# A hybrid attention, scan and expert layer: the decay of the scan's carried states moved from C to the product of states and C

## The chip, the cores and the metric

One core of a Trainium2 chip runs the whole layer in one launch. The metric is the device time of that launch in microseconds (us): the median of three runs for each kernel, and beside it one profiled execution from which every row here is taken. Engines in the rows: PE is TensorE's matmuls, PEld its weight loads, DVE VectorE, ACT ScalarE, POOL GpSimd, SP the queue that issues most of the DMAs.

## The reference

The layer norms 1024 latent and 256 context tokens of width 1024, projects them with one weight `w_in`, runs differential attention and a two-directional Mamba-2 scan (SSD) in parallel, merges the two and ends with a mixture of experts. The change touches the scan alone. For each of 16 heads (64 channels, 4 groups of 4 heads), each chunk and each direction the reference computes

```python
y_diag = einsum('bcign,bcjgn->bcijg', cc, bc) * decay * dtc @ xc          # inside a chunk
y_off  = einsum('bcign,cbgrpn,bcigr->bcigrp', cc, h_prev, exp(acum))      # what earlier chunks carry in
y      = y_diag + y_off                                                   # + d * x, gated by silu(z), group norm
```

`acum` is the running sum of dt times a, `h_prev` the state (128 x 64 for a head) that enters the chunk, and `cc` is C, shared by the four heads of a group. `exp(acum)` depends on head and token i alone, so it may stand at C or at the product of the states and C.

## The kernel before, in words

The program is written out by a list scheduler. `Flow` (class at the top of the listing) keeps a model clock for each engine; pieces of work are Python generators ("streams") with a priority, each `yield` names what the next instructions need, and the stream whose needs are met first by the model is written next. The order of the instructions on every engine is therefore fixed when the kernel is built, from modelled durations; on the chip each engine runs its list in order and waits on semaphores.

`mixer_t` (L791) holds the projections that feed the scan, and the scan. `server` (L947, priority 3, the lowest) multiplies the projections, job by job: dt, 16 convolution tiles, 8 z tiles and 16 gate tiles, three fp32r matmuls of 512 columns for each k into the banks `acc`. It is what PE does when no stream of the scan is ready. `conv_post` and `gate_post` empty those banks on ACT and DVE. When the four convolution tiles of a group of heads are there, `group` (L992) runs, one group at a time, since its buffers `xn`, `Bn`, `hp0`, `hp1` and `CB` exist once:

- transposes of x and B, then `states` (L1050) for the two directions: `xw` on POOL, a matmul, four DVE updates of `hp` for each chunk; then CB = B C for eight chunks.
- four turns (2 pairs of heads x 2 halves of 512 tokens). In each, `unit` (L1080) runs for the two heads hh of the pair: two loads `R[d]` of the cumulated decay (one row of `acd` spread over 128 partitions, 256 KB each), W = mask times dt on DVE (4 + 4 small instructions), G = R[0] - ac on POOL, four DVE instructions that take the minimum with R[1] - ac, W times CB on POOL, exp(G) on ACT, W times G on DVE.
- beside it `decays` (L1129): exp(R[d]) on ACT, then R[d] times C on POOL, for both directions, so four of each in a turn.
- `products` (L1113): for each of four chunks and each head three matmuls into one bank `py`, accumulated there: W against xn, and R[0], R[1] against `hp0`, `hp1`. A head fills 64 of the 128 columns, and each fp32 matmul is two instructions in the trace: 48 in a turn. Model slack: 400 ns after the last of W and R.
- `evac` (L1137): y = d x + py on DVE, y times silu(z) on DVE; `norm` (L1153) after four turns.

Rings: R 6 buffers, W 2, G 2, yt 4, py 2 banks. W is freed by `products`, so the next turn's W starts behind this turn's matmuls. When all four groups are normed, `branches` (L1196) starts to load operands for the branch projections (`bacc` matmuls; `PACE` lets three tiles of 24 matmuls run before attention), and `attention_ahead` (L1326) loads the q and k of attention once five of those operands are there and no job is left.

Of the kernel before, what the change touches and what calls it, by code (L numbers as in the profile page):

```python
# [14 lines left out]
ALU = mybir.AluOpType  # L15
# [4 lines left out]
P = 128  # L20
D = 1024
KC = 8
T = 1024
# [3 lines left out]
LAM_INIT = 0.2  # L27
ND, NR, NDR, NA = 2, 4, 2, 5
LEAD = 2
SLACK = 400.0, 0.0, 200.0, 0.0, 800.0, 400.0, 1500.0  # L30
FG = 3, 3, 2
TAIL = "a0 a1 a2 a3 r0 s0 a4 s1 a5 s2 a6 r1 s3 a7 s4 s5 r2 s6 s7"
# [43 lines left out]
def _n(ap):  # L76
    return ap.tensor.name
# [299 lines left out]
class Layer:  # L377
# [413 lines left out]
    def mixer_t(s):  # L791
        tc, nc, I, F = s.tc, s.nc, s.I, s.F
# [6 lines left out]
        sp = s.open("sp", side="right")  # L799
        pp, pq = s.open("mixps", True), s.open("mixqs", True, side="right")  # L800
        mp = sp
        if True:
            acc = s.ring(pp, [P, 512], "acc", 4)
            aux = s.ring(pq, [P, 512], "aux", 2)
            pys = s.ring(pq, [P, 512], "py", 2)
# [8 lines left out]
            hcs = s.ring(sp, [P, 256], "hc", 2)  # L814
            xws = s.ring(sp, [P, 4, 64], "xw", 2)
            CBs = s.ring(sp, [P, 8, P], "CB", 1)
            Rs = s.ring(sp, [P, 512], "R", 6)
            Gs = s.ring(sp, [P, 4, P], "G", 2)
            Ws = s.ring(sp, [P, 4, P], "W", 2)
            dcol, db = s.dcol, s.db  # L820
            dtn = mp.tile([P, 2, 10, 32], F32, name="dtn")
            dt, dtd = dtn[:, 0], dtn[:, 1]
# [169 lines left out]
            def group(g, x0, x1, B, C):  # L992
                x = (x0, x1)
                yield [lambda: state["dt"], xns, Bns]
                xn, Bn = xns.get(), Bns.get()
                for c in range(0, 10, 2):
                    yield [x0, x1, aux]
                    pt = aux.get()
                    for i in range(2):
                        for q in range(2):  # L1000
                            F.tp(pt[:, (i * 2 + q) * P:(i * 2 + q + 1) * P], x[q][:, (c + i) * P:(c + i + 1) * P], s.ident)
                    yield [pt, "ANY"]
                    F.copy(xn[:, c:c + 2].rearrange("p a b -> p (a b)"), pt)
                    aux.put(pt)
                uxs.put(*x)
                for c in range(0, 10, 4):
                    n = min(4, 10 - c)
                    yield [B, aux]
                    pt = aux.get()
                    for i in range(n):  # L1010
                        F.tp(pt[:, i * P:(i + 1) * P], B[:, (c + i) * P:(c + i + 1) * P], s.ident)
                    yield [pt, "ANY"]
                    F.copy(Bn[:, c:c + n].rearrange("p a b -> p (a b)"), pt[:, :n * P])
                    aux.put(pt)
                yield [hps[0], hps[1], hcs]
                hp = [q.get() for q in hps]
                done, left = [], [16]
                for d in range(2):
                    F.spawn(0, states(g, d, xn, Bn, hp[d], done))
                yield [CBs]  # L1020
                CB = CBs.get()
                for half in range(2):
                    yield [C, B, aux]
                    pt = aux.get()
                    for i in range(4):
                        c = 2 + half * 4 + i
                        F.mm(pt[:, i * P:(i + 1) * P], B[:, c * P:(c + 1) * P], C[:, (c - 2) * P:(c - 1) * P], True, True)
                    yield [pt, "ANY"]
                    F.copy(CB[:, half * 4:half * 4 + 4].rearrange("p a b -> p (a b)"), pt)
                    aux.put(pt)  # L1030
                uBs.put(B)
                yt = {}
                for pair in range(2):
                    for half in range(2):
                        yield [pys]
                        py, ready = pys.get(), []
                        for hh in range(2):
                            yield [(Rs, 2), "NOW"]
                            F.spawn(0, unit(g, pair, half, hh, CB, C, ready))
                        F.spawn(1, products(g, pair, half, xn, hp, py, done, ready, yt))  # L1040
                yield [lambda: len(yt) == 4, "NOW"]
                xns.put(xn)
                Bns.put(Bn)
                for d in range(2):
                    hps[d].put(hp[d])
                CBs.put(CB)
                uCs.put(C)
                yield from norm(g, yt)
# [28 lines left out]
                hcs.put(*hc)  # L1077
                done.append(d)

            def unit(g, pair, half, hh, CB, C, ready):  # L1080

                r = 2 * pair + hh
                h = 4 * g + r
                t0 = 512 * half
                R = [Rs.get(), Rs.get()]
                for d in range(2):
                    F.dma(R[d], bass.AP(tensor=s.acd[d].tensor, offset=s.acd[d].offset + h * T + t0, ap=[[0, P], [1, 512]]))
                Rv = [q.rearrange("p (c i) -> p c i", i=P) for q in R]
                yield [Gs, Ws, "DVE"]
                G, W = Gs.get(), Ws.get()  # L1090
                cs = range(4 * half, 4 * half + 4)
                for c in range(4):
                    F.ts(W[:, c], s.le, dt[:, 2 + cs[c], h:h + 1], None, ALU.mult)
                for c in range(4):
                    F.stt(W[:, c], s.ge, dt[:, 2 + cs[c], 16 + h:16 + h + 1], W[:, c], ALU.mult, ALU.add)
                yield [R[0], "POOL"]
                F.ptt(G, Rv[0], ac[:, 0, 2 + 4 * half:6 + 4 * half, h:h + 1].to_broadcast([P, 4, P]), ALU.subtract)
                yield [G, R[1], "DVE"]
                for c in range(4):
                    F.stt(G[:, c], Rv[1][:, c], ac[:, 1, 2 + cs[c], h:h + 1], G[:, c], ALU.subtract, ALU.min)  # L1100
                k = []
                F.spawn(0, decays(R, C[:, t0:t0 + 512], k, F.clk["DVE"] + 100.0))
                yield [CB, W, "POOL"]
                F.ptt(W, W, CB[:, 4 * half:4 * half + 4], ALU.mult)
                yield [G, "ACT"]
                F.act(G, G, AF.Exp)
                yield [G, "DVE"]
                F.tt(W, W, G, ALU.mult)
                Gs.put(G)
                yield [lambda: len(k) == 2]  # L1110
                ready.append((hh, W, *R))

            def products(g, pair, half, xn, hp, py, done, ready, yt):  # L1113

                yield [lambda: len(done) == 2 and len(ready) == 2]
                yield [hp[0], hp[1], *(F.ready[_n(q)] + 400.0 for v in ready for q in v[1:])]
                for c in range(4):
                    n = 4 * half + c
                    for i, src in enumerate((xn[:, 2 + n], hp[0][:, n], hp[1][:, n])):
                        for v in ready:  # L1120
                            o = 64 * v[0]
                            x = 128 * pair + o
                            F.mm(py[o:o + 64, c * P:(c + 1) * P], src[:, x:x + 64], v[1 + i].rearrange("p c i -> p (c i)")[:, c * P:(c + 1) * P] if i == 0 else v[1 + i][:, c * P:(c + 1) * P], i == 0, i == 2, 134.5)
                for _, W, R0, R1 in ready:
                    Rs.put(R0, R1)
                    Ws.put(W)
                yield from evac(g, pair, half, py, yt)

            def decays(R, C, k, at):  # L1129
                for q in R:  # L1130
                    yield [q, at, "ACT"]
                    F.act(q, q, AF.Exp)
                    yield [q, "POOL"]
                    F.ptt(q, q, C, ALU.mult)
                    k.append(1)

            def evac(g, pair, half, py, yt):  # L1137
                sl = slice(512 * half, 512 * half + 512)
                yield [yts, "NOW"]
                y = yts.get()  # L1140
                F.dma(y, s.xT[2 * g + pair][:, sl])
                yield [y, py, "DVE"]
                F.stt(y, y, dcol[:, 2 * g + pair:2 * g + pair + 1], py, ALU.mult, ALU.add)
                pys.put(py)
                yield [lambda: 2 * g + pair in state["z"], zgs, "NOW"]
                z = zgs.get()
                F.dma(z, s.zs[2 * g + pair][:, sl])
                yield [z, "DVE"]
                F.tt(y, y, z, ALU.mult)
                zgs.put(z)  # L1150
                yt[pair, half] = y
# [192 lines left out]
    def attention(s):  # L1344
        tc, nc, F = s.tc, s.nc, s.F
        ap, pp = s.open("at"), s.open("aps", True)
        if True:
# [20 lines left out]
            def main():  # L1368
# [4 lines left out]
                plan = PLAN.split("|")  # L1373
                for p in range(len(pairs) + LEAD + 1):
                    for j in range(4):
                        for op in plan[j].split():
                            n = p - LEAD * (op[0] != "S") - (op[-1] == "'")
                            if 0 <= n < len(pairs):
# [1122 lines left out]
```

## Time and profile before

| | |
|---|---|
| median of 3 runs | 2750.43 us (2750.11 to 2753.43) |
| profiled execution | 2762.38 us, span in the trace 2760.1 us |
| mean granted TensorE clock | 0.979 of full speed |
| PE busy | 95% of the span |
| DVE, ACT, POOL busy | 73%, 49%, 33% |
| chain that ended last | PE 63%, DMA 8%, DVE 8% |

The profiled execution is 0.4% longer than the median, so a difference worked out from its rows is carried over to the median as it is. The scan lies between about 400 and 1050 us; attention follows to 1500 us, then the merge and the experts.

### The profile page before, as it was taken

The page shows a single profiled execution, that of the slowest core. Times are in us where ns is not written, and L with a number is a line of the kernel's source. Part 1 is how long each engine was busy: PE and PEld are TensorE (multiplying, and loading weights), DVE is VectorE, ACT ScalarE, POOL GpSimd, SP SyncE. Part 2 cuts the span into 40 slices and gives each one's busy share as a digit, 9 for nine tenths or more (in the row PEclk, how much of TensorE's full clock was granted, in tenths as well). Part 3 has the DMA queues.
Part 4 walks back from the last instruction along what each step waited for, and adds up shares of the span by engine and source line. Part 5 has one row for each costly group of instructions (what it writes and reads, how often), then busy time and mean ns, then how long its engine had stood idle before and what let it go on. Part 6 is the DMA issues. An engine that isn't in the chain of part 4 may idle for free.

```text
span 2760.1 us, 41127 instructions
## 1 busy us (share of the span) xinstructions
PE 2610.2 (95%) x14561; PEld 2099.0 (76%) x14561; DVE 2012.4 (73%) x4680; ACT 1341.9 (49%) x2104; POOL 920.9 (33%) x669
## 2 busy tenths in 40 slices
PE   7999999999999998999999999899999999999992
PEld 4888878878787776888888778677787787777771
DVE  6878133777776657888896657877879898888864
ACT  4211113344444446666675432335566666666652
POOL 0111010445354531000000000044667766777761
PEclk9999999999999999999999999999999999999996
DMA  7767253242425345322422872468999999999998
GB/s 275 226 205 220 62 149 102 69 145 77 138 77 149 91 120 186 119 86 87 142 97 75 263 252 107 168 234 288 292 319 315 339 333 311 315 314 307 296 308 251
DMA packets 275409, 545.67 MB, mean 198 GB/s; under 512 B 31562, under 2 KB 166835, under 8 KB 248194
## 3 DMA queue, kind: packets, MB, share of 16 engines
q1 hardware_dynamic: 238178, 432.95, 46.0%
q0 software_dynamic: 35872, 105.88, 14.7%
q10 hardware_dynamic: 1152, 4.19, 0.4%
q8 instruction: 115, 1.88, 0.3%
q14 instruction: 92, 0.75, 0.1%
HBM read 433.78 MB, written 124.73 MB: 202 GB/s over the span
## 4 chain that ended last, share of the span: by engine, by line
PE 63%; DMA 8%; DVE 8%; issue 3%; POOL 2%; ACT 2%; SPq 0%; ACTq 0%; POOLq 0%; DVEq 0%
PE gu L149 18%; PE acc L149 11%; PE dn L149 9%; PE bacc L149 6%; PE sps L149 5%; PE pv L149 4%; PE xt L153 3%; DMA cr<-cumd,crow 2%; PE tr L153 2%; PE aux L149 2%; DVE G L188 2%; DMA qk<-qk 2%; PE py L149 1%; DVE W L181 1%; PE hT L153 1%
## 5 line engine op out<-in xcount | busy, mean ns | idle before, releaser
L149 PE MATMUL acc<-hh,hi 128*128 128x512 f32 (+2 forms) x760 | 304.8, 401 | 1.3 <-DVE ux L188 1.3
L172 DVE TENSOR_TENSOR gl<-raw,gh 128x1024 fp32r<-128x1024 f32 x240 | 288.7, 1218 | 19.7 <-ACT gh L165 19.4
L149 PE MATMUL acc<-hl,hi 128*128 128x512 f32 (+2 forms) x760 | 289.5, 381 | 0.0
L149 PE MATMUL acc<-hh,lo 128*128 128x512 f32 (+1 forms) x736 | 281.0, 382 | 3.0 <-DVE lo L172 3.0
L149 PE MATMUL gu<-gh,xh 128*128 128x512 f32 (+3 forms) x672 | 279.5, 416 | 0.0
L149 PE MATMUL gu<-gh,xl 128*128 128x512 f32 (+3 forms) x672 | 264.6, 394 | 0.0
L149 PE MATMUL gu<-gl,xh 128*128 128x512 f32 (+3 forms) x672 | 264.3, 393 | 0.2 <-DVE gl L172 0.2
L165 ACT CAST gh<-raw 128x1024 fp32r<-128x1024 f32 x240 | 246.0, 1052 | 30.6 <-PE gu L149 21.2
L263 POOL DMA_INDIRECT cr<-cumd,crow x98 | 134.1, 1368 | 319.0 <-DMA wtab<-sc 282.5
L194 DVE TENSOR_SCALAR_CACHE_REDUCE e<-sps 128x512 f32<-128x512 f32 (+1 forms) x384 | 214.4, 597 | 33.9 <-PE sps L149 33.6
L269 POOL DMA_INDIRECT yacc<-y,tk x98 | 189.4, 1933 | 80.8 <-DMA yacc<-y,tk 14.4
L149 PE MATMUL sps<-qk 128*128 128x512 f32 (+1 forms) x768 | 196.1, 387 | 11.2 <-DMA qk<-qk 6.1
L157 ACT ACTIVATE e<-e,st 128x1280 f32<-128x1280 f32 x128 | 174.8, 1366 | 31.8 <-DVE st L203 31.6
L263 POOL DMA_INDIRECT wc<-wtab,tk x98 | 153.8, 1570 | 86.5 <-DVE tk L183 58.3
L149 PE MATMUL acc<-hi,hh 128*128 128x512 f32 x448 | 182.0, 406 | 0.0
L149 PE MATMUL acc<-hi,hl 128*128 128x512 f32 x448 | 176.6, 394 | 0.4 <-DVE hl L172 0.4
L149 PE MATMUL acc<-lo,hh 128*128 128x512 f32 x448 | 176.6, 394 | 0.0
L149 PEld LDWEIGHTS sps<-qk 128*128 128x128 f32 x768 | 141.4, 192 | 43.9 <-DVE e L194 9.8
L149 PEld LDWEIGHTS acc<-hh,hi 128*128 128x128 f32 (+1 forms) x760 | 142.5, 187 | 32.7 <-issue 4.2
L149 PE MATMUL pv<-wr,vv 128*128 128x256 f32 x640 | 164.6, 380 | 0.0
L149 PEld LDWEIGHTS acc<-hh,lo 128*128 128x128 f32 x736 | 138.8, 189 | 32.9 <-DVE lo L172 4.0
L149 PEld LDWEIGHTS acc<-hl,hi 128*128 128x128 f32 (+1 forms) x760 | 142.6, 188 | 27.4 <-issue 0.8
(327 smaller groups left out, 6246.5 us busy)
## 6 DMA issues: line engine op xcount, KB each, us to landing
raw<-in_w_e_gate_dram SPq DMA_DIRECT2D x64, 1024.0 KB, 9.2
raw<-in_w_e_up_dram SPq DMA_DIRECT2D x64, 1024.0 KB, 11.4
draw<-in_w_e_down_dram SPq DMA_DIRECT2D x64, 1024.0 KB, 9.9
qk<-qk POOLq DMA_DIRECT2D x16, 1664.0 KB, 10.4
raw<-in_w_in_dram SPq DMA_DIRECT2D x40, 512.0 KB, 4.7
wada<-in_w_ada_dram SPq DMA_DIRECT2D x32, 512.0 KB, 5.6
R<-acd SPq DMA_DIRECT2D x64, 256.0 KB, 5.4
qk<-sa SPq DMA_DIRECT2D x52, 256.0 KB, 4.1
```

Of the source, the lines that this page charges most:

```text
L149: s.nc.tensor.matmul(out, l, r, start=start, stop=stop)
L153: s.nc.tensor.transpose(out, in_, ident)
L157: s.nc.scalar.activation(out, in_, fn, **kw)
L165: s.nc.scalar.copy(out, in_)
L172: s.nc.vector.tensor_tensor(out, a, b, op=op)
L181: s.nc.vector.tensor_scalar(out, a, s1, s2, op0=op0)
L188: s.nc.vector.scalar_tensor_tensor(out, a, sc, b, op0=op0, op1=op1)
L194: s.nc.vector.tensor_scalar(out, a, s1, None, op0=op0, op1=op1, accum_out=acc)
L263: s.nc.gpsimd.indirect_dma_start(out=out, out_offset=None, in_=table, in_offset=bass.IndirectOffsetOnAxis(ap=idx, axis=0), **kw)
L269: s.nc.gpsimd.indirect_dma_start(out=table, out_offset=bass.IndirectOffsetOnAxis(ap=idx, axis=0), in_=in_, in_offset=None, compute_op=ALU. ...
```

## The change

The exponential of the decay is loaded once for a pair of heads (row of head 0 on partitions 0 to 63, of head 1 on 64 to 127), and multiplied by the product of states and C after the matmul, on DVE out of PSUM. A new stream `carried` does this; `decays` goes. `products` keeps only W against xn, asks no longer for the states, takes its bank `py` late, and has a model slack of 1200 ns in place of 400. R is given back right after G is made. The tiles E of `carried` come out of the ring of R (`Es` is the same ring), the size of the ring W is named NW and stays 2.

```diff
-            Rs = s.ring(sp, [P, 512], "R", 6)
+            Rs = Es = s.ring(sp, [P, 512], "R", 6)
@@ group, in each turn
-                        yield [pys]
-                        py, ready = pys.get(), []
+                        ready, box = [], []
+                        yield [(Es, 2), "NOW"]
+                        F.spawn(0, carried(g, pair, half, hp, C, done, box, [Es.get(), Es.get()]))
                         for hh in range(2):
                             yield [(Rs, 2), "NOW"]
-                            F.spawn(0, unit(g, pair, half, hh, CB, C, ready))
-                        F.spawn(1, products(g, pair, half, xn, hp, py, done, ready, yt))
+                            F.spawn(0, unit(g, pair, half, hh, CB, ready, [Rs.get(), Rs.get()]))
+                        F.spawn(1, products(g, pair, half, xn, ready, box, yt))
@@ unit, after G is made
-                k = []
-                F.spawn(0, decays(R, C[:, t0:t0 + 512], k, F.clk["DVE"] + 100.0))
+                Rs.put(*R)
...
-                yield [lambda: len(k) == 2]
-                ready.append((hh, W, *R))
+                ready.append((hh, W))
+            def products(g, pair, half, xn, ready, box, yt):
+                yield [lambda: len(ready) == 2]
+                yield [pys, xn, *(F.ready[_n(W)] + 1200.0 for _, W in ready)]
+                py = pys.get()
                 for c in range(4):
+                    for hh, W in ready:
+                        o = 64 * hh
+                        F.mm(py[o:o + 64, c * P:(c + 1) * P], xn[:, 2 + 4 * half + c, 128 * pair + o:128 * pair + o + 64], W[:, c], True, True, 134.5)
...
+            def carried(g, pair, half, hp, C, done, box, E):
+                h, t0 = 4 * g + 2 * pair, 512 * half
+                for d in range(2):
+                    F.dma(E[d], bass.AP(tensor=s.acd[d].tensor, offset=s.acd[d].offset + h * T + t0, ap=[[T, 2], [0, 64], [1, 512]]))
+                for q in E:
+                    yield [q, "ACT"]
                     F.act(q, q, AF.Exp)
+                yield [lambda: len(done) == 2]
+                for d in range(2):
+                    yield [hp[d], C, pys]
+                    py = pys.get()
+                    for c in range(4):
+                        F.mm(py[:, c * P:(c + 1) * P], hp[d][:, 4 * half + c, 128 * pair:128 * pair + 128], C[:, t0 + c * P:t0 + (c + 1) * P], True, True, 218.0)
+                    yield [py, E[d], "DVE"]
+                    F.tt(E[d], py, E[d], ALU.mult)
+                    pys.put(py)
+                yield [*E, "POOL"]
+                F.ptt(E[0], E[0], E[1], ALU.add)
+                Es.put(E[1])
+                box.append(E[0])
@@ evac, after y = d x + py
+                yield [lambda: len(box) == 1]
+                yield [y, box[0], "DVE"]
+                F.tt(y, y, box[0], ALU.add)
+                Es.put(box[0])
```

## Rows read from the trace of the kernel before

**Rows 1.** Part 1 of the page: TensorE's busy time.

```profile
PE 2610.2 (95%) x14561; PEld 2099.0 (76%) x14561; DVE 2012.4 (73%) x4680; ACT 1341.9 (49%) x2104; POOL 920.9 (33%) x669
```

**Rows 2.** Windows: stretch, its length, busy time (instructions) by engine, clock, DMA share, GB/s.

```profile
517.00:597.00 80.00, 72.49 (x475) 59.69 (x474) 70.19 (x148) 44.96 (x62) 49.67 (x34) 0.98 0.33 94
650.00:732.00 82.00, 76.14 (x485) 62.78 (x483) 71.67 (x141) 45.86 (x64) 47.41 (x31) 0.96 0.35 109
784.00:873.00 89.00, 84.68 (x541) 69.83 (x540) 73.85 (x149) 49.65 (x68) 51.13 (x35) 0.98 0.39 118
920.00:1000.00 80.00, 72.19 (x432) 58.16 (x430) 60.73 (x120) 44.05 (x60) 47.09 (x30) 0.96 0.38 109
...
597.00:650.00 53.00, 53.00 (x273) 44.76 (x271) 28.25 (x96) 12.43 (x21) 14.04 (x21) 1.00 0.36 118
```

**Rows 3.** Waits, 391 to 1050 us: total us, times, longest.

```profile
POOL G L176 <- DMA R<-acd: 15.3, 9, 3.9
...
PE py L149 <- DVE W L172: 14.1, 8, 2.6
...
DVE W L181 <- PE py L149: 11.1, 6, 5.2
...
PE py L149 <- POOL R L176: 7.3, 9, 3.3
```

**Rows 4.** POOL's timeline at the end of the scan: the first loads for attention.

```profile
1041.50 1.82 POOL L228 DMA_DIRECT2D qk<-qk  x3
```

**Rows 5.** By tile, 1000 to 1120 us: count, ns min/median/max, first and last start.

```profile
L149 PE MATMUL bacc<-bxh,bwh x12: 389/389/503, 1035.1 to 1054.4; 128*128 128x512 f32 x12
...
L149 PE MATMUL sps<-qk x138: 274/394/796, 1055.1 to 1119.7; 128*128 128x512 f32 x92, 128*128 128x256 f32 x46
```

**Rows 6.** The window before attention, branch matmuls (`bacc`) alone, columns as in rows 2.

```profile
1048.00:1056.00 8.00, 7.29 (x33) 5.67 (x31) 0.00 (x0) 1.00 1.04 409
```

**Rows 7.** Groups by line and form, 391 to 1050 us: busy, mean ns, idle before.

```profile
L176 POOL TENSOR_TENSOR R<-R,uC 128x512 f32<-128x512 f32 x64 | 91.6, 1447 | 24.5 <-ACT R L157 16.4 <-DVE yt L188 3.5 <-DVE lo L172 1.8
L188 DVE SCALAR_TENSOR_TENSOR G<-R,ac,G 128x128 f32<-128x128 f32 x128 | 77.9, 671 | 8.4 <-POOL G L176 8.4
...
L157 ACT ACTIVATE R<-R 128x512 f32<-128x512 f32 x64 | 39.6, 624 | 8.4 <-POOL G L176 5.6 <-DVE G L188 2.5
...
L172 DVE TENSOR_TENSOR yt<-yt,zg 128x512 f32<-128x512 f32 x16 | 11.5, 722 | 7.1 <-DMA zg<-zs 6.9
...
L176 POOL TENSOR_TENSOR G<-G 128x512 f32<-128x512 f32 x8 | 10.3, 1286 | 38.7 <-ACT G L157 38.7
...
L149 PE MATMUL aux<-uC,uB 128*128 128x128 f32 x64 | 8.4, 275 | 0.0
```

**Rows 8.** Timeline of DVE and POOL inside one turn: start, us, instructions.

```profile
675.89 1.13 DVE L188 SCALAR_TENSOR_TENSOR G<-R,ac,G 128x128 f32<-128x128 f32 x4
...
681.52 5.27 DVE L188 SCALAR_TENSOR_TENSOR G<-R,ac,G 128x128 f32<-128x128 f32 x4 [0.94 <-POOL G L176]
...
681.45 2.59 POOL L176 TENSOR_TENSOR R<-R,uC 128x512 f32<-128x512 f32 x2
684.00 1.35 POOL L176 TENSOR_TENSOR W<-W,CB 128x512 f32<-128x512 f32 x1
685.31 1.33 POOL L176 TENSOR_TENSOR R<-R,uC 128x512 f32<-128x512 f32 x1
```

**Rows 9.** PE's timeline: one chunk of `products`, and the eight instructions of one CB.

```profile
554.49 0.59 PE L149 MATMUL py<-R,hp 128*64 128x128 f32 x6
...
555.14 0.59 PE L149 MATMUL py<-R,hp 128*64 128x128 f32 x6
...
513.58 1.05 PE L149 MATMUL aux<-uC,uB 128*128 128x128 f32 x8
```

**Rows 10.** A product of a bank and a tile on DVE, in the branches (500 to 1400 us).

```profile
L172 DVE TENSOR_TENSOR braw<-bacc,braw 128x512 f32<-128x512 f32 x7 | 4.8, 684 | 0.0
```

More of the change, by code (lines that the diff above doesn't have):

```diff
@@ L29 @@
 LEAD = 2
+NW = 2
 SLACK = 400.0, 0.0, 200.0, 0.0, 800.0, 400.0, 1500.0
@@ L816, in mixer_t @@
             CBs = s.ring(sp, [P, 8, P], "CB", 1)
-            Rs = s.ring(sp, [P, 512], "R", 6)
+            Rs = Es = s.ring(sp, [P, 512], "R", 6)
             Gs = s.ring(sp, [P, 4, P], "G", 2)
-            Ws = s.ring(sp, [P, 4, P], "W", 2)
+            Ws = s.ring(sp, [P, 4, P], "W", NW)
             dcol, db = s.dcol, s.db
@@ L1078, in states, with unit @@
                 done.append(d)
-            def unit(g, pair, half, hh, CB, C, ready):
+            def unit(g, pair, half, hh, CB, ready, R):
                 r = 2 * pair + hh
@@ L1084, in unit @@
                 t0 = 512 * half
-                R = [Rs.get(), Rs.get()]
                 for d in range(2):
@@ L1109, in unit @@
                 Gs.put(G)
-                yield [lambda: len(k) == 2]
-                ready.append((hh, W, *R))
-            def products(g, pair, half, xn, hp, py, done, ready, yt):
-                yield [lambda: len(done) == 2 and len(ready) == 2]
-                yield [hp[0], hp[1], *(F.ready[_n(q)] + 400.0 for v in ready for q in v[1:])]
-                for c in range(4):
[L1118 to L1125, printed above, removed]
-                    Ws.put(W)
-                yield from evac(g, pair, half, py, yt)
@@ L1129, in decays @@
-            def decays(R, C, k, at):
-                for q in R:
-                    yield [q, at, "ACT"]
-                    F.act(q, q, AF.Exp)
[L1133 to L1137, printed above, removed]
+                ready.append((hh, W))
[3 more added lines that the diff above has]
+                py = pys.get()
+                for c in range(4):
+                    for hh, W in ready:
+                        o = 64 * hh
+                        F.mm(py[o:o + 64, c * P:(c + 1) * P], xn[:, 2 + 4 * half + c, 128 * pair + o:128 * pair + o + 64], W[:, c], True, True, 134.5)
+                for _, W in ready:
+                    Ws.put(W)
+                yield from evac(g, pair, half, py, box, yt)
@@ L1138, in evac @@
+            def evac(g, pair, half, py, box, yt):
                 sl = slice(512 * half, 512 * half + 512)
```

## The prediction

> **What bounds the kernel now.** I read the page first: PE is busy 95% of the span [rows 1], so what counts is PE's idle time and PE's clock. Then the windows by stage: the scan has four stretches of turns, one for each group of heads, and between them the transposes and states. In the latter PE is busy for all of its 53 us at clock 1.00; in the four turn windows it is idle for 7.5, 5.9, 4.3 and 7.8 us, 25.5 in all, and the granted clock is 0.96 to 0.98 [rows 2]. [...]
>
> The waits say for what PE stands idle there: 14.1 us at `py` for W on DVE, in 8 waits, and 7.3 us at `py` for R on POOL, in 9 [rows 3]. PE's list was laid out by the model, DVE and POOL come later than the model thinks, and PE meets them at `py` in each turn. The timeline of one turn shows why: four instructions that make G take 1.13 us when POOL is quiet and 5.27 us when POOL has R times C twice, W times CB and R times C to do; each waits for one POOL product [rows 8]. Over all turns the G instructions take 77.9 us [rows 7] where 32 x 1.13 = 36.2 would do: 41.7 us of DVE time lost behind POOL.
>
> A second bound runs beside PE: the chain of groups. Its end starts the branch operands and the load of q and k, issued at 1041.5 [rows 4]; the first scores start at 1055.1 [rows 5]. PE fills that time with gate jobs and then with branch matmuls, 36 of the 72 that the pacing allows (12 of each of three kinds, one kind in [rows 5]). At 7.29 us for 33 [rows 6] the other 36 are worth 8 us. So if PE gains G and the chain of groups grows by X, the kernel gains the smaller of G and 8 - X: with too little cover PE waits for q and k.
>
> **The change part by part.** *PE's work* stays. A chunk of `products` is 12 instructions, 0.65 us from one start to the next [rows 9], so a turn's 48 take 2.6 us. After, 16 of them remain, 0.87 us, and `carried` adds 8 fp32 matmuls over the full 128 columns, 16 instructions. Eight like them, in CB, took 1.05 us [rows 9], and one by itself shows 0.275 [rows 7], so seven starts take 0.775, 0.11 each, and 16 of them 1.77 us a turn. Two heads side by side in 64 columns cost what one product over 128 costs: 2.6 us again, +0.4 us over 16 turns.
>
> *POOL* loses 64 products R times C, 91.6 us, and gets 16 sums, at 1.29 us from the sum G + G: 20.6 us [rows 7]. *ACT* loses half of 39.6 us of exponentials [rows 7]; it was waiting in most turns, so this buys nothing by itself. *SP* issues 32 more loads of 256 KB, 8.4 MB beside a DMA share of 0.33 to 0.39 [rows 2]; the bandwidth is there. But SP is one queue, and the tiles come from the six R buffers: in a turn E takes two, and one of them is held until y has been summed, while R is given back right after G instead of after `products`. The wait of POOL for R, 15.3 us in 9 [rows 3], may go or double; I leave it.
>
> *DVE* gets three instructions a turn: two products of a bank and a tile, 0.684 us by the branches' row [rows 10], and y + E, 0.722 by y times z, two tiles in SBUF [rows 7]. That is 16 x (2 x 0.684 + 0.722) = 33.4 us. Against it stands the relief from POOL: three of the four POOL products in front of the stretched G are R times C [rows 8], three quarters of 41.7 is 31 us; the 16 new sums can take at most 20.6 back. Bounds 10 and 31, I take 25, since a sum comes once a turn and mostly not in front of G.
>
> By the row, emptying a bank costs DVE 0.684 us and the number of banks emptied in the turns goes from 16 to 48. [...]
>
> *The chain, X.* DVE is idle 9.8, 10.3, 15.1 and 19.3 us in the turn windows, 54.5 in all [rows 2], so added work can vanish there: of 33.4 I put half on the chain, 17. The relief takes 25 off. DVE's wait for W's buffers behind `py`, 11.1 us [rows 3], shrinks as the turn's last matmuls fall from 2.6 to 0.87 us and R no longer has to arrive: -7. The slack of 1200 in place of 400 ns holds W back by 0.8 us a turn, 12.8 us if always felt; half, +6. X = 17 - 25 - 7 + 6 = -9, with bounds -36 (all in the gaps, relief whole) and +35 (none in the gaps, no relief). 8 - X is 17.
>
> *PE's gain, G.* The wait for R goes: 7.3. The wait for W is met by 0.8 us more of slack in each of its 8 places: 6.4 of 14.1 (bounds 0 and 14.1). With 13.7 of 25.5 us idle gone, the clock's 9.9 us fall by the same share, 5.3 (bounds 0 and 9.9). Against it: work +0.4, and a wait that the trace doesn't have: three users of the two `py` banks in a turn in place of one, each freed by DVE. Behind a matmul of `carried` that waits for a bank stands all of PE's list. Bounds 0 and another 14.1 (the nearest row, PE behind DVE at `py`); `carried` may run early in the turn, before W is ready, so I take 4. G = 7.3 + 6.4 + 5.3 - 0.4 - 4 = 14.6, below the 17 that the chain allows.
>
> The sum stands against the profiled execution, 2762.4 us, which is 12 us above the median: 2747.8 there, 2735.8 in the median, say 2736.
>
> **The rivals.** *First, nothing (about 2747).* The model drops R's POOL work from its own turn too, so PE's `py` moves earlier together with DVE's real end, and the waits only change their names: W's 14.1 stays, R's 7.3 becomes 4 at the banks, the clock stays. 3 us gained. For it: the model prices none of the 41.7 us, before or after. Against it: most of the unpriced time is tied to the very instructions that go. Late loads of R (15.3 once more, X = +6) end here as well.
>
> *Second, all of it (about 2719).* With POOL quiet, DVE keeps the model's pace and PE never waits at `py`: 21.4 + 9.9 = 31.3 us. It needs X below -23. Against it: W times CB, G and the sums still stand between DVE's instructions.
>
> *Third, slower (about 2761): DVE becomes the bound of the turns.* Place: DVE's list in a turn, from the first W to y + E. Relief only 10, since the sums and y + E take the lock's place; 6 of 33.4 us in gaps; slack felt whole, 12.8; the wait behind `py` gone, -11: X = 33.4 - 6 - 10 + 12.8 - 11 = +19, so 8 - X = -11. It decides from X = +8 on, half a us a turn; then groups end so late that PE runs out of gate jobs and of paced branch matmuls and waits for q and k. For it: DVE is busy 88% of the first turn window [rows 2]. Against it: the gaps of 54.5 us. [...]
>
> **How the numbers follow.** A measurement here tells about 0.2%, 5.5 us, from no change. Forecast 0.48 (its own range 2726 to 2744), second rival 0.12, both faster: 0.60. First rival 0.22: same. Third 0.18: slower. The range goes from the second rival, 2719, to 2757, which takes in the first and the near part of the third; some 0.1 is left above it and 0.05 to 0.1 below.
>
> **What would show it.** Right: no PE wait for POOL's R, below 10 us for W; the groups of G on DVE at 50 us or less in place of 77.9; POOL some 70 us less busy; idle PE in the turn windows at about 12 us with the clock nearer 1; q and k issued at about 1030. Wrong: new waits of PE for a `carried` product at `py` of 10 us or more, G still stretched, turn stretches longer than 80 us, or PE idle just before the first scores.

## The result and the profile after

The changed kernel takes 2797.23 us (median of 4 runs, 2791.51 to 2803.31), against 2751.93 us for the kernel before on the same chip: ratio 1.0158, interval 1.0141 to 1.0174. It is 45 us slower where 15 us of gain were forecast, and outside the range. The profiled execution of the changed kernel took 2791.51 us, 29 us more than that of before (2762.38); the rows are read against those 29, not against the 45 of the medians, since the profiled execution of before was the slowest of its kernel, that of after the fastest. Line numbers are higher by one (L173 is before's L172).

Part 1 of the page after, to be read beside [rows 1]: DVE, ACT and POOL are less busy, PE is busy 9.5 us longer with 256 instructions fewer (its clock is lower, as the windows below show), and the span is 29.7 us longer.

```profile
span 2789.8 us, 40641 instructions
...
PE 2619.7 (94%) x14305; PEld 2109.1 (76%) x14305; DVE 2005.2 (72%) x4729; ACT 1327.1 (48%) x2075; POOL 835.0 (30%) x621
```

The windows of the four stretches of turns, columns as in [rows 2]:

```profile
517.00:601.00 84.00, 77.64 (x433) 64.78 (x432) 66.67 (x154) 39.02 (x51) 25.73 (x20) 0.96 0.37 109
655.00:765.00 110.00, 94.18 (x488) 77.87 (x487) 72.85 (x172) 45.67 (x60) 31.94 (x23) 0.91 0.38 115
808.00:925.00 117.00, 106.69 (x567) 89.05 (x566) 81.90 (x191) 53.34 (x71) 31.62 (x26) 0.91 0.41 123
957.00:1045.00 88.00, 76.23 (x393) 62.63 (x392) 61.94 (x141) 45.21 (x58) 26.48 (x19) 0.92 0.42 126
```

The stretches take 399 us in place of 331. PE is idle for 44.3 us of them (25.5 before), and the clock's shortfall, each stretch's length times what its granted clock lacks to 1.00, is 30.8 us (9.9 before, from [rows 2]). DVE has not become the bound: its idle time in the turns went from 54.5 to 115.6 us. The waits of 391 to 1100 us say on whom the engines wait now, beside [rows 3]:

```profile
DVE W L173 <- ACT G L158: 50.7, 13, 8.3
...
ACT R L158 <- DMA R<-acd: 39.7, 10, 6.4
...
PE py L150 <- DVE R L173: 28.8, 6, 6.2
POOL G L177 <- DMA R<-acd: 28.5, 5, 9.9
...
PE py L150 <- DVE W L173: 7.6, 2, 6.4
```

Read upwards from the DMA: ACT waits 39.7 us for loads of E (the tiles of E bear the ring's name R), POOL 28.5 us for loads of R. DVE waits 50.7 us for exp(G) on ACT, where it had waited 6.3 us before. PE waits 28.8 us at `py` for DVE's product with E. One turn's timeline shows the links, rows of POOL, SP, ACT, DVE and PE (start, us):

```profile
540.60 1.10 POOL L177 TENSOR_TENSOR G<-R,ac 128x512 f32<-128x512 f32 x1
...
541.72 0.51 SPq L214 DMA_DIRECT2D R<-acd  x1
...
553.28 0.63 ACT L158 ACTIVATE R<-R 128x512 f32<-128x512 f32 x1 [3.87 <-DMA R<-acd]
553.82 0.61 ACT L158 ACTIVATE G<-G 128x512 f32<-128x512 f32 x1
...
554.53 0.69 DVE L173 TENSOR_TENSOR W<-W,G 128x512 f32<-128x512 f32 x1 [5.93 <-ACT G L158]
555.14 0.68 DVE L173 TENSOR_TENSOR R<-py,R 128x512 f32<-128x512 f32 x1
...
555.88 1.98 PE L150 MATMUL py<-W,xn 128*64 128x128 f32 x16 [5.18 <-DVE R L173]
```

A load of E goes out at 541.72, when POOL has made its G of the unit before (its end is 541.70), and E's exponential starts 11.6 us later. exp(G) stands right behind it in ACT's list, so W waits on DVE, the product with E waits behind W, and PE waits for the bank that this product frees.

Most of those 11.6 us are the load's own. By the updates of its semaphore in the trace it has landed at 553.17, 11.45 us after its issue. In the changed kernel the 32 loads of E land after 7.1 to 12.2 us (median 8.4), the 64 of R after 3.0 to 12.0 (median 4.9), though both move 256 KB; the kernel's model gives either 2.9 us (lines of `_dma`: 256 KB at 360 bytes a ns, and 2.2 us).

The end of the scan, beside [rows 4, 5], by tile, 1050 to 1095 us:

```profile
L150 PE MATMUL sps<-qk x7: 281/396/767, 1089.8 to 1094.5; 128*128 128x512 f32 x5, 128*128 128x256 f32 x2
L229 POOL DMA_DIRECT2D qk<-qk x3: 536/573/726, 1081.7 to 1083.0; - x3
```

q and k are issued 40 us later than before and the scores start 35 us later, so the loss is there when attention begins; at the end of the profiled execution 29 us of it are left.

### The profile page after: what moved, and what is told of

Same layout as the page of the kernel before. It is cut to its first block, busy times and chain, and to the rows that moved or that the text cites. A ratio compares the mean times of both kernels' runs of the same rounds, so it can differ in the third digit from the quotient of the medians.

```text
span 2789.8 us, 40641 instructions
## 1 busy us (share of the span) xinstructions
PE 2619.7 (94%) x14305; PEld 2109.1 (76%) x14305; DVE 2005.2 (72%) x4729; ACT 1327.1 (48%) x2075; POOL 835.0 (30%) x621
## 5 line engine op out<-in xcount | busy, mean ns | idle before, releaser
L150 PE MATMUL acc<-hh,hi 128*128 128x512 f32 (+2 forms) x760 | 313.1, 412 | 1.8 <-DVE ux L189 1.8
L173 DVE TENSOR_TENSOR gl<-raw,gh 128x1024 fp32r<-128x1024 f32 x240 | 288.7, 1217 | 23.1 <-ACT gh L166 22.8
L150 PE MATMUL sps<-qk 128*128 128x512 f32 (+1 forms) x768 | 196.2, 387 | 12.2 <-DMA qk<-qk 7.5
L158 ACT ACTIVATE e<-e,st 128x1280 f32<-128x1280 f32 x128 | 174.7, 1366 | 33.4 <-DVE st L204 33.3
```

What stands on the lines that cost most here:

```text
L150: s.nc.tensor.matmul(out, l, r, start=start, stop=stop)
L158: s.nc.scalar.activation(out, in_, fn, **kw)
L173: s.nc.vector.tensor_tensor(out, a, b, op=op)
```

## Experiments

The kernel before ran on every chip beside these; its medians there were 2770.39, 2753.31, 2771.02 and 2753.02 us, so ratios are compared. Three theories were put against each other: L, the loads of E come late; B, three users are too many for two `py` banks; D, DVE's new work lies on the chain.

**Without the loads of E** (first run, on the changed kernel; E is then made from dt, which leaves the decay of the carried states out, and the run tells of the time alone):

```diff
-                for d in range(2):
-                    F.dma(E[d], ...)
                 for q in E:
-                    yield [q, "ACT"]
-                    F.act(q, q, AF.Exp)
+                    yield [q, dtn, "ACT"]
+                    F.act(q, dtn.rearrange("p a c h -> p (a c h)")[:, :512], AF.Exp)
```

> The changed kernel, but E is the exponential of a tile that lies in SBUF anyway (dt), so the 32 loads of E are left out and nothing waits for them; all other instructions, buffers and banks stay. Theory L (the loads of E come late: their buffers come free only when the turn before has made its G, and the exponential of E then stands in ACT's list ahead of that of G): most of the 45 us go, 2750 to 2765 us, and PE's wait at py for the product with E falls from 28.8 us to under 8. Theory B (three users of two py banks, freed by a busy DVE): nothing changes, 2785 to 2800, the wait stays. Theory D (the 33 us of new DVE work lie on the chain): the same, 2785 to 2800.

Measured: 0.9934 (0.9912 to 0.9957), faster than before by what was forecast for the change. Banks, users, DVE's instructions and the six buffers are the same as in the changed kernel, so B and D fall for the kernel as it stands. Its waits (391 to 1130 us), and the window of the scan:

```profile
PE py L150 <- DVE R L173: 5.4, 5, 2.0
...
DVE W L173 <- ACT G L158: 7.0, 10, 1.6
...
POOL G L177 <- DMA R<-acd: 3.9, 1, 3.9
...
505.00:1000.00 495.00, 481.52 (x2597) 399.02 (x2596) 366.53 (x929) 214.35 (x298) 158.42 (x149) 1.00 0.38 113
```

Of the three waits 3.9 to 7.0 us are left (28.5 to 50.7 in the changed kernel), R's loads are in time but for one, and the clock is 1.00. A turn still takes six tiles of six here, at 0.9934 of before. So a full ring by itself costs nothing here; it cost where tiles were held for loads on their way, 1.0158 in the changed kernel and 1.0210 in the kernel before with four buffers (below).

**The dose**: one direction's load left out, 16 of 32 (`E[1]` from dt as above, and its exponential listed first; `E[0]` loaded).

> Dose: the changed kernel with the load of E for one direction left out (its E is the exponential of dt, as in the run without any), 16 loads of E in place of 32. Theory L: between the run without (0.9934) and the changed kernel (1.0158), 0.998 to 1.010. If a load of E stalls a turn however few there are, 1.012 to 1.016.

Measured: 1.0000 (0.9985 to 1.0014), between 0.9934 and 1.0158, as L has it. The first 16 loads cost 0.66%, the second 16 another 1.58%, each by the ratio to before on its own chip.

**The slack.** `+ 1200.0` back to `+ 400.0` in `products`.

> The changed kernel with the slack of products back at 400 ns. If the slack of 1200 held W back on the chain (0.8 us in 16 turns), it gains up to 13 us: 2785. Theory L: PE's wait for W grows by what the slack hid and the loads stay late, 2795 to 2805.

Measured: 1.0141 (1.0122 to 1.0161), not told from the changed kernel: the slack isn't the loss.

**The model told of the load** (`yield [F.ready[_n(q)] + 4000.0, "ACT"]` ahead of E's exponential), and **the units' buffers first** (the two `unit` streams are spawned ahead of `carried`, which takes its E after them):

> The changed kernel, but the model waits 4 us longer for the loads of E before it lists their exponential, so that this stands later in ACT's list and the products with E later in DVE's and PE's. Theory L: the other work no longer stands behind a load that is late, a part of the 45 us goes, 2760 to 2780, though the buffers stay short. Theories B and D: no change beyond 5 us (2790 to 2800).

> The changed kernel, but a turn takes the buffers of its two units first and those of E after them, so that R's loads go out ahead of E's. If it is the order of the loads in front of a turn (E delays R and stands ahead of G on ACT), a good part goes: 1.000 to 1.008 of before. If it is that six buffers are short for six loads in any order, it stays at 1.012 to 1.020.

Measured: 1.0171 (1.0148 to 1.0193) and 1.0190 (1.0173 to 1.0207). Neither gains; L's prediction for the first was wrong. The waits moved: told, ACT waits 11.0 us for E and POOL 47.9 us for R; units first, POOL not at all and ACT 49.2 us. With six buffers a later E holds its buffers longer, and somebody's load is late in either order; the ring of eight below bears on that.

**The shortage put into the kernel before**: `"R", 6` becomes `"R", 4`, so that a turn needs all there are.

> The kernel before with a ring of 4 R in place of 6, so that a turn needs all buffers there are, as in the changed kernel (6 of 6): the loads of the next turn wait for this turn's end. Theory L: it gets slower by 15 to 40 us, with POOL's wait for R far above the 15.3 us of before. Theories B and D, by which the loads are no matter: within 5 us of before, 2747 to 2757.

Measured: 1.0210 (1.0190 to 1.0229), with no part of the change in it. Its waits for R (391 to 1130 us):

```profile
POOL G L176 <- DMA R<-acd: 107.3, 21, 12.7
...
DVE G L188 <- DMA R<-acd: 22.6, 8, 4.4
```

**Two buffers more.** One uC (the tile that holds a group's C) in place of two makes room for them in SBUF. Four runs set the scale: before with one uC, the changed kernel with one uC, that with `"R", 8`, and that without E's loads; a fifth adds the model's longer wait to the ring of 8.

> The kernel before with one uC: what the room for two more R buffers costs by itself. With the loads of E left out and with the ring of 8 below it gives the scale. 1.01 to 1.03 of before.

> Control for the next: the changed kernel with one uC in place of two, which makes room for two more R buffers. A group's C can then be loaded into only when the group before is through; 1.015 to 1.03 of before.

> The control with one uC (1.0444) without the loads of E (E from dt, as in the first run). Theory L: the whole excess over the kernel before with one uC goes, and a little more: at or below that kernel's ratio. The ring of 8 (1.0327) lies between the two; how near says how much of it is shortage of buffers.

> The control with a ring of 8 R: a turn needs six, two are free to be loaded ahead. Theory L, by shortage of buffers: 0.5 to 1.2% below the control, and the waits for the loads fall from some 70 us to under 40. If the loads are late by SP's queue or their own length alone, no more than 0.3% below the control.

> One uC, a ring of 8 R, and the model waits 4 us longer for E's loads. If shortage of buffers is what made the longer wait useless with six (1.0171), it is useful with eight: ACT's wait for E falls from 69 us to under 25 without POOL's wait for R coming back, and the time falls 0.5 to 1.2% below the ring of 8 alone (1.0327), to 1.02 to 1.028. If E's wait on ACT is harmless, no change (1.030 to 1.036).

| with one uC | ratio | interval |
|---|---|---|
| before | 1.0226 | 1.0206 to 1.0245 |
| changed | 1.0444 | 1.0423 to 1.0464 |
| changed, no loads of E | 1.0252 | 1.0235 to 1.0269 |
| changed, ring of 8 | 1.0327 | 1.0303 to 1.0350 |
| changed, ring of 8, model told | 1.0287 | 1.0269 to 1.0304 |

The runs were on two chips (E from R, below, gave 0.9955 and 0.9966 on two). The loads of E cost 1.92% here (1.0444 less 1.0252); two more buffers give 1.17 of it back. R's loads are then in time (POOL waits 4.3 us, 32.6 with six), but ACT still waits 68.9 us for E. Told of the load, ACT waits 8.1 us and another 0.40% comes back, less than the 0.5 expected, with the two intervals just touching. The same telling gave nothing with six. So the shortage is the larger price; the wait of E's exponential for its long load is the smaller and less sure one, and telling the model helped only where buffers were there. 0.35% stays without an account.

Without E's loads the changed kernel is no faster than before under one uC (L expected it at or below 1.0226), against 0.66% with two. Its trace shows where: from 1010 us the turns of the last group run with hardly a projection left to cover them. The first line is its window there, the second that of before with one uC:

```profile
1010.00:1070.00 60.00, 21.38 (x137) 18.29 (x137) 55.04 (x124) 12.03 (x19) 27.26 (x20) 0.62 0.25 76
...
1010.00:1065.00 55.00, 27.02 (x209) 21.66 (x210) 45.97 (x84) 20.66 (x29) 36.75 (x26) 0.74 0.28 82
```

DVE is busy 55.0 of 60 us, so by the trace theory D holds there: the added work does lie on the chain. With two uC projections remain for PE during the last group's turns, and this doesn't show.

**E without loads of its own.** Both heads' R are in SBUF on all partitions, so E can be made from them in R's own tiles:

```diff
-                        yield [(Es, 2), "NOW"]
-                        F.spawn(0, carried(..., [Es.get(), Es.get()]))
+                        rs = {}
+                        F.spawn(0, carried(..., rs))
@@ unit, after G
-                Rs.put(*R)
+                rs[hh] = R
@@ carried
+                yield [lambda: len(rs) == 2]
+                at, E = F.clk["DVE"] + 100.0, rs[0]
                 for d in range(2):
+                    yield [E[d], rs[1][d], at, "ACT"]
+                    F.act(E[d][:64], E[d][:64], AF.Exp)
+                    F.act(E[d][64:], rs[1][d][64:], AF.Exp)
+                    Rs.put(rs[1][d])
```

> The same sum as the changed kernel, without loads or buffers of its own for E: once both heads' G are made, the exponentials of R are written half by half (partitions 0 to 63 from the first head's R, 64 to 127 from the second's) into the first head's R tiles, which become E; four exponentials a turn on ACT, as before. Loads are 64 again and a turn needs four buffers of six. Theory L: as fast as the run without the loads of E, 0.992 to 0.997 of before. Theories B and D: 1.01 or more, as the changed kernel.

> E from R's tiles once more, on the chip of the two runs beside it: 0.994 to 0.997 of before.

Measured: 0.9955 (0.9939 to 0.9971), and 0.9966 (0.9956 to 0.9976) in five rounds on another chip. This computes the whole layer and beats both kernels, by 0.3 to 0.5% of before. Two settings of it, on the second chip:

> E from R's tiles, but the model may list their exponentials only 1.5 us after G is made, so that exp(G) stands ahead of them on ACT. If they stood ahead of G's, this is 3 to 8 us faster than E from R (0.9955): 0.992 to 0.994; otherwise the same within 3 us.

> E from R's tiles with the slack of products at 400 ns. If 1200 is right for PE's list, PE's wait for W grows and it is 3 to 10 us slower than E from R: 0.997 to 1.000; if it only holds W back, it is as much faster.

Measured: 0.9984 (0.9972 to 0.9996) with E's exponentials 1.4 us later by the model, 1.0000 (0.9985 to 1.0015) with the slack of 400. Later is no gain; the slack of 1200 is worth 0.3% once the loads are out of the way, which the kernel as changed couldn't show.

## Why the prediction was wrong

**The step that failed** stands in the part on SP: "The wait of POOL for R, 15.3 us in 9, may go or double; I leave it". It had just said that E takes two of the six R buffers and that the bandwidth is there. Counted on, a turn takes six tiles of six, so a load of the next turn goes out only when a tile of this one is given back; the rows held loads of R that already came late with four of six. And a load of E was taken for one of R, while it lands after 8.4 us in the median where R's takes 4.9. POOL's wait was put into the first rival as X = +6. Measured, POOL's wait became 28.5 us (the forecast's "double", so its size was named and then left out of the sum), and ACT got one of 39.7 us that the prediction didn't have: E's exponential is one of the instructions that the change issues, and whose work stands behind it on ACT (exp(G), so W, so `py`) was never asked. With the loads alone taken out, the time is 0.9934 of before in place of 1.0158.

**The wait at the banks** was sized 4 us with bounds up to 14.1, and came out at 28.8. Three users of two banks were suspected, but without the loads the same users wait 5.4 us there: the size came from DVE standing behind a late E, not from the number of banks. (Under one uC, with the last turns uncovered and DVE busy for 55.0 of 60 us, 27.8 us of it stay without the loads.)

**The rest of the sum held in its parts.** R's wait at PE went (7.3 to none), W's fell from 14.1 to 7.6 us (7.7 were left in the sum). DVE's new work was sized 33.4 us: 21.9 + 11.0 measured. The relief of G was sized 25 us and measured 19.6: with less POOL work the instructions that make G took 58.3 us in place of 77.9 [rows 7], above the 50 that was to show the forecast right, and 52.8 in the run with E from R. (POOL is not quiet throughout the 1.13 us of [rows 8]: its W times CB starts 0.22 us into them. The third rival's "lock" is a word for the stretched G of [rows 8], four instructions of 1.37 us beside POOL's products of 1.29 to 1.35; how the two engines hold each other up is not shown beyond these times.) The groups of the changed kernel:

```profile
L189 DVE SCALAR_TENSOR_TENSOR G<-R,ac,G 128x128 f32<-128x128 f32 x128 | 58.3, 515 | 2.0 <-POOL G L177 2.0
...
L173 DVE TENSOR_TENSOR R<-py,R 128x512 f32<-128x512 f32 x32 | 21.9, 686 | 11.6 <-PE py L150 6.3 <-ACT R L158 2.5 <-issue 2.4
...
L173 DVE TENSOR_TENSOR yt<-yt,R 128x512 f32<-128x512 f32 x16 | 11.0, 688 | 0.3
```

The 9.9 us of the clock in the sum are an estimate from [rows 2], each window's length times what its clock lacks to 1.00 (1.6 + 3.3 + 1.8 + 3.2); no run shows that 5.3 of them go with 13.7 us of idle time. In their place the changed kernel's windows came to 30.8; without the loads of E the clock was 1.00 from 505 to 1000 us, where the kernel before had 0.98 from 505 to 1017.

POOL's busy time fell by 86 us over the span (71 forecast). Without the loads the first run measured 0.66% (0.43 to 0.88) against 0.53% forecast. Part of that nearness is luck: its waits for W (1.0 us) and its clock (1.00) came out better than the sum had them, its waits at the banks worse (7.4 us, two of them for DVE's y, in place of 4).

**The bound by the chain of groups.** X was -9 in the forecast and +40 measured (q and k at 1081.7 in place of 1041.5), so 8 - X is -32 us. PE's own side, G, is about -40 by the windows: 18.8 us more idle and 20.9 us more lost clock. The profiled executions differ by 29. Both sides have the sign, and the smaller of the two, which the prediction would take, says 11 us too much.

**The rivals.** The slower side was taken, but not by the third rival: DVE is busy for 71% of the turns (84% before), and without the loads of E the 48 banks emptied by DVE alone ran at 0.9934 of before; only in the uncovered turns under one uC is DVE busy for 55.0 of 60 us. The first rival named the late loads and priced them at 15 us of waiting, where ACT and POOL together wait 68 us for them.

## What to carry to other kernels

When a change takes new tiles from a ring that is there, count the tiles that one round of the loop takes against the ring: where it takes them all, a load of the next round goes out only when a tile of this one comes back, and a load that is slow to land holds its tile and delays the others (POOL's wait for R went from 15.3 to 28.5 us here). Read from the trace how long the new load itself takes to land; one of the same size beside it need not take as long (8.4 and 4.9 us in the median for 256 KB). Then ask of each load what stands behind its first user in that engine's list (exp(G) here: ACT waited 39.7 us for E, and DVE 50.7 us for exp(G)). If the data already lies in SBUF in another tile, try to make the new tile from that one: here it ran at 0.9955 of before, with the load at 1.0158, though the DMA share in the turns had been 0.33 to 0.39.

## What was not expected of the hardware

The lower clock weighed more than before: behind 25.5 us of idle PE stood 9.9 us of lost clock, behind 44.3 us stood 30.8. In the second to fourth stretch the granted clock was 0.91 to 0.92. The trace has it at 0.50 of full speed nine times in the four stretches, 6.8 us each, and at 1.00 between: 1.00 from 545 to 555 us, 0.50 from 556 to 561, 1.00 from 563 to 573. Eight of the nine begin in the last 3.0 us of a wait of PE at `py` (3.4 to 6.4 us, all that are longer than 1.2 us there), the ninth at the end of a wait of 2.2 us for POOL's G. In the kernel before there are four of 3.4 us and one of 6.8. In the run without E's loads the clock was 1.00 over 505 to 1000 us.

Two loads of 256 KB differ in how they land. E's load reads two rows and spreads each over 64 partitions, R's spreads one row over 128. A load of R has 16 updates of its semaphore, a load of E three: of the one issued at 541.72 they come at 542.70, 552.54 and 553.17. Of the load of R issued at 542.40 fourteen came by 548.64, the last two at 553.18 and 553.82, right behind E's. From 551 to 553 us, with the last updates of these two and of one more load of R to come, the DMA share is 0.13, at 50 GB/s. In the kernel before, which has no loads of E, R's land after 3.3 to 8.1 us (median 5.6); without E's loads POOL waits for one load of R, 3.9 us, in place of five and 28.5 us. Why a load of E lands later than one of R, and whether it holds up the R load behind it, is not shown. No run gives E's load another form, for example two loads of one row each, so how much of the 45 us is the form of the load and how much the six buffers is open; under one uC two more buffers gave back 1.17 of 1.92%.
